# A fixed order of TensorE's instructions for the attention units of a hybrid layer

## The chip, the cores and the metric

The kernel runs on one core of a Trainium2 chip. The metric is device time in microseconds (us), the median over several runs; lower is better. One core has five engines that matter here: TensorE (PE, matmuls and transposes), VectorE (DVE), ScalarE (ACT), GpSimd (POOL) and SyncE (SP, which issues the DMAs). Each takes its instructions in the order in which the program lists them.

## The reference

One layer with four token mixers beside each other, over 640 tokens: 512 latent tokens, which see 128 cached context tokens and themselves, and 128 prompt tokens, which see only themselves. Cut to what matters:

```python
h = _rmsnorm(x, P['norm_mix_pre']) * (1 + sc1) + sh1
u = _split_cols(h @ P['w_in'])
o_a, st_a = _hgrn_mixer(u, P, lb_f, lb_b, ctx)
o_b, st_b = _swa_mixer(u, P, pos, ctx)     # windowed, 8 heads, 2 kv heads, a sink logit
o_c, st_c = _mla_mixer(u, P, pos, ctx)     # latent, 8 heads, key = 64 + 32 rotary
o_d, st_d = _gqa_mixer(u, P, pos, ctx)     # grouped, 8 heads, 2 kv heads
y = _merge((o_a, o_b, o_c, o_d), u['gates'], P)
...
# each attention: softmax(scale * q k^T) v, with the maximum taken off
# _merge: sum over branches of (o_n @ w_branch[n]) * sigmoid(gates_n), then @ w_out
```

Then the modulated MLP. Everything is float32.

## The kernel before, in words

Float32 products are made of three matmuls of a rounded high part and a rest (`wh`, `wl`, `hTh`, `hTl`), so one projection block is three lines, L365 to L367 or L381 to L383. After the start and the recurrent mixer come, in this order, windowed attention (branch 1), grouped attention (branch 3) and latent attention (branch 2), the merge, and the MLP.

Attention is done in units: two heads by 128 query rows. `unit` (L800) writes one whole unit. With 640 keys it takes each of the two heads in turn: scores into a tile `sc` of two PSUM banks (matmuls L949 and L950, in latent attention also L1182), the row maximum on VectorE (L818), the exponential with its sum on ScalarE (L819), the reciprocal on VectorE (L821) and the scaling of P on GpSimd (`weigh`, L809). With fewer keys both heads share the two banks and one reduce (L835, L840, L847). Then TensorE transposes P by pairs of key blocks (L856) into tiles `tp`, which ScalarE and VectorE copy out in turn (L858, L860) to `PT`; the products with V (L1009, in latent attention L1185) go into a tile `pv`, and `o_evac` (L504) splits it into a high part `oh` on ScalarE and a rest `ol` on VectorE. `tp` and `pv` share one pool of two PSUM banks, `pst`; the scores have `pss`, two times two banks; everything else has `psm`, two banks.

`run_gqa` (L990) does windowed and grouped attention: 20 units in two halves, with a query projection (`queries`, L906) ahead of each half; behind it `gates` (L699) makes the branch's sigmoid gates, 8 blocks of two times 24 matmuls, with a sigmoid on ScalarE after the fourth and the eighth. `merge` (L967) stands behind the gates of the branch. In `mla` (L1033) each of four head pairs has a projection of its queries, transposes of the rotary part (L1152), for every second pair the values, a projection of its keys, and then five units; after each unit three `side_steps`, pieces of the modulation (`ada`, L211) whose weights come by DMA. During latent attention `psm` is closed and its two banks hold `ada_ps` and one buffer `pj`. The unit with 128 keys is the one of the prompt.

What order the engines get is not what the code lists: outside of `in_order` (L71) a scheduler with its own timeline places each engine's instructions, so that a unit's parts stand between gates, projections and other units. Inside `in_order(PE)`, which the recurrent mixer already uses, TensorE keeps the order of the code.

## Time and profile before

| | us |
|---|---|
| median of 3 runs | 1500.1 |
| lowest, highest | 1498.42, 1501.73 |
| profiled execution, its own time | 1502.2 |
| its span | 1500.4 |
| TensorE busy | 1430.5 (95% of the span) |
| VectorE, ScalarE, GpSimd busy | 796.1, 481.4, 432.2 |
| mean granted TensorE clock | 0.991 |

TensorE's time counts matmuls and their modelled ends, so short gaps do not show as idle. A row of a timeline gives the start, the duration, the engine, line and operation, the tiles out and in, and in brackets the idle time before it with what ended it. "x4" in such a row is a run of four. A granted clock of 1.00 is 2.4 GHz, 0.50 is 1.2 GHz.

### The profile page before, as it was taken

How to read it: one execution, taken by the hardware profiler on the slowest of the kernel's cores; microseconds unless marked ns; L12 is line 12 of the kernel's file. 1: busy time of each engine (PE TensorE's matmuls, PEld its weight loads, DVE VectorE, ACT ScalarE, POOL GpSimd, SP SyncE). 2: the span in 40 equal slices, each digit the busy share in tenths (PEclk: the TensorE clock that was granted, in tenths of full speed). 3: DMA queues.
4: the chain of work that ended last, by engine and by line, in shares of the span. 5: the costliest groups of instructions: out<-in, count | busy, mean ns of one | idle time of the engine just before them, and what ended most of it. 6: DMA issues, size and time to landing. Idle time of an engine off the chain costs nothing.

```text
span 1500.4 us, 26709 instructions
## 1 busy us (share of the span) xinstructions
PE 1430.5 (95%) x10969; PEld 1302.2 (87%) x10969; DVE 796.1 (53%) x1447; ACT 481.4 (32%) x1161; POOL 432.2 (29%) x456
## 2 busy tenths in 40 slices
PE   6999999899999999999998998998999999999996
PEld 5898998899898998999996677988898998898995
DVE  4347657476643788433725566746243444444446
ACT  4334333333443235442124565225220110110112
POOL 2015325243321545222213334124111111112114
PEclk9999999999999999999999999999999999999998
DMA  9421212121112131112224601221343223222221
GB/s 328 128 85 58 70 49 64 50 68 50 45 43 59 34 84 37 33 42 74 80 68 143 224 15 43 99 85 56 112 129 101 80 71 98 71 70 71 75 66 70
DMA packets 138225, 121.17 MB, mean 81 GB/s; under 512 B 22296, under 2 KB 119412, under 8 KB 138104
## 3 DMA queue, kind: packets, MB, share of 16 engines
q1 hardware_dynamic: 138104, 119.47, 26.4%
q8 instruction: 86, 1.41, 0.4%
q14 instruction: 35, 0.29, 0.1%
HBM read 115.96 MB, written 3.49 MB: 80 GB/s over the span
## 4 chain that ended last, share of the span: by engine, by line
PE 70%; issue 13%; DVE 8%; POOL 5%; ACT 2%; DMA 1%; POOLq 0%; DVEq 0%; SPq 0%; ACTq 0%
PE mm L365 12%; PE mm L366 11%; PE mm L367 11%; PE mm L381 4%; PE mm L382 4%; PE mm L383 4%; PE tp L856 3%; POOL wh L139 3%; PE pv L1009 3%; PE sc L383 3%; PE sc L381 2%; PE sc L382 2%; PE sc L949 2%; PE sc L950 2%; DVE wl L142 1%
## 5 line engine op out<-in xcount | busy, mean ns | idle before, releaser
L139 POOL TENSOR_SCALAR wh<-wr 128x1024 fp32r<-128x1024 f32 (+3 forms) x136 | 156.7, 1154 | 536.4 <-PE mm L366 290.4
L142 DVE TENSOR_TENSOR wl<-wr,wh 128x1024 fp32r<-128x1024 f32 (+3 forms) x160 | 198.9, 1247 | 160.0 <-POOL wh L139 120.8
L365 PE MATMUL mm<-hTh,wh 128*128 128x320 f32 x704 | 220.5, 313 | 2.0 <-DVE qA L520 0.9
L367 PE MATMUL mm<-hTh,wl 128*128 128x320 f32 x704 | 219.2, 311 | 0.0
L366 PE MATMUL mm<-hTl,wh 128*128 128x320 f32 x704 | 218.2, 310 | 0.0
L366 PE MATMUL mm<-h2Tl,wh 128*128 128x320 f32 x512 | 159.4, 311 | 1.1 <-DVE h2Tl L142 1.1
L365 PE MATMUL mm<-h2Th,wh 128*128 128x320 f32 x512 | 159.5, 312 | 0.0
L367 PE MATMUL mm<-h2Th,wl 128*128 128x320 f32 x512 | 159.2, 311 | 0.0
L809 POOL TENSOR_SCALAR P<-P,rden 128x640 f32<-128x640 f32 (+3 forms) x120 | 84.5, 713 | 184.0 <-DVE rden L821 80.7
L365 PEld LDWEIGHTS mm<-hTh,wh 128*128 128x128 f32 x704 | 132.2, 188 | 3.9 <-DVE qA L520 1.0
L367 PEld LDWEIGHTS mm<-hTh,wl 128*128 128x128 f32 x704 | 132.2, 188 | 0.9 <-issue 0.7
L366 PEld LDWEIGHTS mm<-hTl,wh 128*128 128x128 f32 x704 | 132.2, 188 | 0.5 <-issue 0.3
L382 PE MATMUL mm<-wl,hidh 128*128 128x512 f32 x320 | 124.8, 390 | 0.6 <-DVE wl L142 0.6
L381 PE MATMUL mm<-wh,hidh 128*128 128x512 f32 x320 | 125.3, 392 | 0.0
L383 PE MATMUL mm<-wh,hidl 128*128 128x512 f32 x320 | 124.6, 389 | 0.0
L1292 ACT ACTIVATE relu<-mm 128x320 f32<-128x320 f32 x64 | 28.0, 438 | 281.1 <-PE mm L367 281.1
L366 PEld LDWEIGHTS mm<-h2Tl,wh 128*128 128x128 f32 x512 | 97.1, 190 | 1.7 <-DVE h2Tl L142 1.5
L365 PEld LDWEIGHTS mm<-h2Th,wh 128*128 128x128 f32 x512 | 96.9, 189 | 0.7 <-issue 0.4
L367 PEld LDWEIGHTS mm<-h2Th,wl 128*128 128x128 f32 x512 | 97.0, 189 | 0.0
L1293 DVE TENSOR_TENSOR relu<-relu 128x320 f32<-128x320 f32 x64 | 40.4, 632 | 100.8 <-ACT relu L1292 100.8
L1305 DVE TENSOR_TENSOR y<-mm,y 128x512 f32<-128x512 f32 x70 | 48.2, 689 | 81.9 <-PE mm L383 81.9
L381 PE MATMUL sc<-wh,hTh 128*128 128x256 f32 (+2 forms) x224 | 72.0, 322 | 5.5 <-DVE tx L935 2.4
(355 smaller groups left out, 3238.4 us busy)
## 6 DMA issues: line engine op xcount, KB each, us to landing
wr<-in_w_in SPq DMA_DIRECT2D x56, 512.0 KB, 3.7
wada<-in_w_ada SPq DMA_DIRECT2D x48, 512.0 KB, 4.5
wr<-in_w_mlp_in SPq DMA_DIRECT2D x32, 512.0 KB, 4.0
wr<-in_w_mlp_out SPq DMA_DIRECT2D x32, 512.0 KB, 3.6
wr<-in_w_in SPq DMA_DIRECT2D x64, 64.0 KB, 2.1
wr<-in_w_branch SPq DMA_DIRECT2D x8, 512.0 KB, 4.1
wr<-in_w_branch SPq DMA_DIRECT2D x16, 256.0 KB, 4.1
wr<-in_w_out SPq DMA_DIRECT2D x8, 512.0 KB, 3.6
```

The lines of the kernel that those rows point to most:

```text
L139: G.tensor_scalar(out=out, in0=src, scalar1=1.0, scalar2=1.0, op0=ALU.mult, op1=ALU.mult)
L142: V.tensor_tensor(out=out, in0=src, in1=f(hi), op=ALU.subtract)
L365: PE.matmul(out=ps[:, 0:tn], lhsT=wh, rhs=a, start=(k == 0), stop=False)
L366: PE.matmul(out=ps[:, 0:tn], lhsT=wh, rhs=b, start=False, stop=False)
L367: PE.matmul(out=ps[:, 0:tn], lhsT=wl, rhs=a, start=False, stop=(k == nk - 1))
L381: PE.matmul(out=ps[:, 0:n], lhsT=a, rhs=w[k][0], start=(start and k == 0), stop=False)
L382: PE.matmul(out=ps[:, 0:n], lhsT=a, rhs=w[k][1], start=False, stop=False)
L383: PE.matmul(out=ps[:, 0:n], lhsT=b, rhs=w[k][0], start=False, stop=(stop and k == nk - 1))
L809: G.tensor_scalar(out=Pt[:, i, 0:W], in0=Pt[:, i, 0:W], scalar1=rden[:, i:i + 1], scalar2=1.0, op0=ALU.mult, op1=ALU.mult)
L856: PE.transpose(out=tp[:, kk, i], in_=Pt[:, i, 128 * (kt + kk):128 * (kt + kk) + 128], identity=ident)
L1009: PE.matmul(out=out, lhsT=Vt[:, ks[kt], 64 * a:64 * a + 64], rhs=PTa, start=start, stop=stop)
L1305: V.tensor_tensor(out=ys, in0=ps, in1=ys, op=ALU.add)
```

## The change

- `unit` no longer writes its parts one after the other. It returns four functions: the first half's scores (`wide(0)`, or both halves), the second half's (`wide(1)`), the transposes in two parts (`turn`), and the products.
- `run_units` writes TensorE's order by hand, inside `in_order(PE)`. One step has the first scores of unit u, the products of unit u-2, fill, the second scores of u, transposes of u-1 (tiles 0 and 1), fill, transposes of u-1 (tile 2).
- `Fill` hands out other work by shares. In `run_gqa` the fill is the second query projection and the gates, mixed; a query transpose comes one half of a gate block after its projection. The gates are no longer behind the units.
- In `mla` all scores use one tile `scores` of three banks with one buffer: the first head of a unit in columns 0 to 639, the second in 640 to 1279. The pieces are 512+128 and 384+256 columns instead of 320+320. The projections of the next head pair are the fill beside the units of the present one, in two buffers `pj`; those of the first pair come ahead. `side_steps` are two a unit instead of three.

The core of the diff; the class `Fill`, the pools and `mla`'s inner functions, which move without change, are left out:

```diff
-        if W > 512:
-
-            for i in range(2):
-                sv = sc_tile()[:, :, 0:W // 2]
+        def wide(i):
+            if banks is None:
+
+                sv, to = sc_tile()[:, :, 0:W // 2], Pt[:, i, 0:W].rearrange("p (a n) -> p a n", a=2)
                 for a in range(2):
                     score(sv[:, a], i, a * (W // 2), W // 2)
...
+            else:
+                sv, to = banks[:, W * i:W * i + W], Pt[:, i, 0:W]
+                k0 = 0
+                while k0 < W:
+                    kn = min(W - k0, 512 - (W * i + k0) % 512)
+                    score(sv[:, k0:k0 + kn], i, k0, kn)
+                    k0 += kn
...
+        def turn(part):
+            for j, kt in list(enumerate(range(0, nk, 2)))[2 * part:2 * part + 2]:
+                kn = min(2, nk - kt)
+                tp = tp_tile().rearrange("p (k i) t -> p k i t", i=2)
+                for i in range(2):
+                    for kk in range(kn):
+                        PE.transpose(out=tp[:, kk, i], in_=Pt[:, i, 128 * (kt + kk):128 * (kt + kk) + 128], identity=ident)
+                if j % 2 == 0:
+                    S.activation(out=PT[:, kt:kt + kn], in_=tp[:, 0:kn], func=AF.Copy)
+                else:
+                    V.tensor_copy(out=PT[:, kt:kt + kn], in_=tp[:, 0:kn])
...
+        if W > 512:
+            return lambda: wide(0), lambda: wide(1), turn, products
+        return both, lambda: None, turn, products
+
+    def run_units(units, beside, after=lambda: None):
+
+
+        cur = old = None
+        units = iter(units)
+        with in_order(PE):
+            while True:
+                new = next(units, None)
+                if new is None and cur is None and old is None:
+                    break
+                if new:
+                    new[0]()
+                if old:
+                    old[3]()
+                    after()
+                beside()
+                if new:
+                    new[1]()
+                if cur:
+                    cur[2](0)
+                beside()
+                if cur:
+                    cur[2](1)
+                old, cur = cur, new
...
+        def dense():
+
+            gate = gate_steps(n, sig)
+            for i, share in enumerate(second):
+                yield share
+                if i % 2 == 0:
+                    yield next(gate)
+            yield from gate
...
+        fill = Fill(dense())
+        run_units(units(), lambda: fill.give(0.5))
+        fill.rest()
+        return sig
...
+        scores = psx.tile([128, 3, 512], F32, name="scores").rearrange("p a n -> p (a n)")
...
+        preludes = [None] + [heads(jj, got[jj], lambda: psx.tile([128, 512], F32, tag="pj", name="pj", bufs=2))
+                             for jj in range(1, 4)]
...
+        run_units(units(), lambda: fill.give(0.4), lambda: side_steps(2))
```

How this stands in the engines' orders, at three places. (`x3` is a run of three; a wait names the engine waited for; the numbers tell one buffer's use from the next.)

TensorE in grouped attention, before: the transposes of a unit. `tp_6267` is its first tile, `tp_6273` the second, `tp_6279` the third; the lines 949 and 950 are scores, 381 to 383 gates.

```order
L856 MATMUL tp_6267<-ident_82,P_6247 128x128 [waits Pool_49]
L856 MATMUL tp_6267<-ident_82,P_6247 128x128
L949 MATMUL sc_6352<-K_5397,Q_5663 128x320 [waits Activation_49]
L950 MATMUL sc_6352<-K_5397,Q_5663 128x320
...
L383 MATMUL mm_6685<-wh_6681,hTl_140 128x256
L381 MATMUL mm_6685<-wh_6681,hTh_138 128x256
L856 MATMUL tp_6273<-ident_82,P_6247 128x128 [waits Activation_49]
L856 MATMUL tp_6273<-ident_82,P_6247 128x128 x3
L856 MATMUL tp_6279<-ident_82,P_6247 128x128 [waits DVE_49]
L856 MATMUL tp_6279<-ident_82,P_6247 128x128
```

Scores of the next units and gates stand between the first tile's transposes and the second's.

TensorE in grouped attention, the change: `pv_6443` are products of unit u-2, `sc_6456` the second scores of u, `tp_6465` and `tp_6471` the first two tiles of u-1; the lines 365 to 367 are fill.

```order
L1081 MATMUL pv_6443<-PT_6198,Vt_5399 64x128 [waits Activation_49]
L1081 MATMUL pv_6443<-PT_6198,Vt_5399 64x128
L1002 MATMUL sc_6456<-K_5397,Q_5663 128x320
...
L872 MATMUL tp_6465<-ident_82,P_6345 128x128 [waits PE_49,Pool_49]
L872 MATMUL tp_6465<-ident_82,P_6345 128x128
L872 MATMUL tp_6465<-ident_82,P_6345 128x128 [waits Pool_49]
L872 MATMUL tp_6465<-ident_82,P_6345 128x128
L872 MATMUL tp_6471<-ident_82,P_6345 128x128 [waits Activation_49]
L872 MATMUL tp_6471<-ident_82,P_6345 128x128 x3
L365 MATMUL mm_6477<-hTh_137,wh_6312 128x320 [waits DVE_49]
L366 MATMUL mm_6477<-hTl_139,wh_6312 128x320
```

The second tile's transposes follow the first's at once, and wait for ScalarE.

ScalarE in grouped attention, the change, around the sigmoid of the first half of the gates (L711): `sig_6192` are the gates, L832 is the exponential, L520 is `oh`, L874 the copy of transposed tiles.

```order
L708 ACTIVATE sig_6192<-mm_7185 128x320 [waits PE_49]
L874 ACTIVATE PT_7085<-tp_7211 128x256 [waits PE_49]
L711 ACT_TABLE_LOAD
L711 ACTIVATE sig_6192<-sig_6192 128x2560 [waits Activation_49]
L832 ACT_TABLE_LOAD [waits DVE_49]
L832 ACTIVATE P_7218,den_7216<-sc_7220,negm_7215 128x640 [waits Pool_49]
L520 ACTIVATE oh_5395<-pv_7229 128x128 [waits PE_49]
L874 ACTIVATE PT_7149<-tp_7251 128x512 [waits PE_49]
L832 ACTIVATE P_7218,den_7216<-sc_7242,negm_7215 128x640 [waits DVE_49]
```

The sigmoid now stands between two table loads in the middle of the units, and behind it are the exponential of the next unit, the evacuation of products and the copy of transposed tiles.

TensorE in latent attention, the change: one step. `scores_9116` is the one tile of three banks, `pv_9269` products, L211 `ada`, `tp_9304` to `tp_9316` the three tiles of the unit before.

```order
L1002 MATMUL scores_9116<-mK_9083,mQ_9005 128x512 [waits Activation_49]
...
L1275 MATMUL scores_9116<-ckv_7858,mQ_9005 128x128
L1278 MATMUL pv_9269<-PT_9122,qv_8938 64x128 [waits DVE_49]
...
L211 MATMUL ada_ps_9117<-wada_9282,cpad_120 32x256 [waits DMAHW5_49]
L211 MATMUL ada_ps_9117<-wada_9282,cpad_120 32x256 x3
L1002 MATMUL scores_9116<-mK_9083,mQ_9005 128x384 [waits Activation_49]
...
L1275 MATMUL scores_9116<-ckv_7858,mQ_9005 128x256
L872 MATMUL tp_9304<-ident_82,P_9188 128x128 [waits PE_49,Pool_49]
...
L872 MATMUL tp_9310<-ident_82,P_9188 128x128 [waits DVE_49]
L872 MATMUL tp_9316<-ident_82,P_9188 128x128 [waits Activation_49]
L1002 MATMUL scores_9116<-mK_9083,mQ_9005 128x512 [waits Activation_49]
```

Both halves' scores are written into one tile, and each half's first matmul waits for ScalarE; products and ada steps stand between the first pair, transposes between the second.

## Rows read from the trace of the kernel before

**Rows 1.** Busy time by stage: us, PE, PEld, DVE, ACT, POOL, PEclk, DMA share, GB/s:
```profile
326.00:500.00 174.00, 168.54 (x1291) 153.95 (x1290) 97.26 (x239) 69.40 (x192) 51.67 (x71) 1.00 0.20 51
500.00:685.00 185.00, 181.35 (x1483) 172.05 (x1482) 114.00 (x250) 74.21 (x188) 67.98 (x78) 0.99 0.19 49
812.00:814.00 2.00, 2.00 (x13) 1.19 (x12) 0.96 (x2) 1.90 (x3) 0.29 (x1) 0.50 0.47 184
882.00:912.00 30.00, 24.70 (x207) 20.73 (x206) 20.76 (x47) 17.96 (x48) 14.83 (x23) 1.00 0.06 19
```

**Rows 2.** Instruction groups of PE, 326 to 500: count, busy, mean ns, idle before:
```profile
L856 PE MATMUL tp<-ident,P 128*128 128x128 f32 x120 | 20.1, 281 | 0.7 <-ACT PT L858 0.7
```

**Rows 3.** The same view, 500 to 685:
```profile
L856 PE MATMUL tp<-ident,P 128*128 128x128 f32 x168 | 25.8, 280 | 1.1 <-DVE ol L142 1.0 <-ACT PT L858 0.2
L1009 PE MATMUL pv<-PT,Vt 128*64 128x128 f32 x336 | 23.0, 279 | 1.6 <-ACT PT L858 1.6
```

**Rows 4.** Timeline of PE in windowed attention: start, duration, operation, idle before:
```profile
391.32 0.66 PE L856 MATMUL tp<-ident,P 128*128 128x128 f32 x4
392.73 0.44 PE L856 MATMUL tp<-ident,P 128*128 128x128 f32 x2 [0.75 <-ACT PT L858]
```

**Rows 5.** Timeline of PE in grouped attention:
```profile
590.99 0.66 PE L856 MATMUL tp<-ident,P 128*128 128x128 f32 x4
591.40 0.39 PE L949 MATMUL sc<-K,Q 128*128 128x320 f32 x1
...
592.40 0.66 PE L856 MATMUL tp<-ident,P 128*128 128x128 f32 x4 [0.17 <-ACT PT L858]
```

**Rows 6.** Timeline of ACT around a sigmoid:
```profile
438.80 1.28 ACT L697 ACT_TABLE_LOAD   x1
440.09 2.34 ACT L697 ACTIVATE sig<-sig 128x2560 f32<-128x2560 f32 x1
442.33 0.26 ACT L506 ACTIVATE oh<-pv 128x128 fp32r<-128x128 f32 x1
```

**Rows 7.** Timeline of PE in latent attention, products:
```profile
903.04 1.31 PE L1185 MATMUL pv<-PT,mVt 128*64 128x128 f32 x20 [0.72 <-ACT PT L858]
904.28 0.66 PE L856 MATMUL tp<-ident,P 128*128 128x128 f32 x4
...
910.25 0.88 PE L1185 MATMUL pv<-PT,mVt 128*64 128x128 f32 x12
911.05 0.44 PE L856 MATMUL tp<-ident,P 128*128 128x128 f32 x2
```

**Rows 8.** Timeline of all engines in latent attention, one half-unit:
```profile
890.52 0.79 ACT L819 ACTIVATE P<-sc,negm 128x640 f32<-128x640 f32 x1 [2.17 <-DVE negm L818]
...
891.46 0.41 PE L949 MATMUL sc<-mK,mQ 128*128 128x320 f32 x1
...
892.30 0.31 PE L1182 MATMUL sc<-ckv,mQ 128*128 128x320 f32 x1
...
892.65 0.82 DVE L818 TENSOR_REDUCE negm<-sc 128x1 f32<-128x640 f32 x1 [0.53 <-PE sc L1182]
...
893.57 0.80 ACT L819 ACTIVATE P<-sc,negm 128x640 f32<-128x640 f32 x1 [0.32 <-DVE rden L821]
```

**Rows 9.** Timeline of PE, the start of latent attention:
```profile
806.44 0.41 PE L949 MATMUL sc<-mK,mQ 128*128 128x320 f32 x1
...
810.38 0.63 PE L1182 MATMUL sc<-ckv,mQ 128*128 128x320 f32 x1 [0.58 <-POOL mQ L139]
810.82 0.47 PE L949 MATMUL sc<-mK,mQ 128*128 128x320 f32 x1
811.08 0.47 PE L950 MATMUL sc<-mK,mQ 128*128 128x320 f32 x1
```

**Rows 10.** Instruction groups of PE by form, 806 to 942, merge beside the units:
```profile
L365 PE MATMUL mm<-oh,wh 128*128 128x320 f32 x11 | 3.7, 335 | 1.4 <-DVE G L1206 1.4
```

**Rows 11.** Timeline of PE, the last products of latent attention:
```profile
941.90 0.44 PE L1185 MATMUL pv<-PT,qv 128*64 128x128 f32 x4
```

More of the change, by code (lines that the diff above doesn't have):

```diff
@@ L496, in trunk, with __init__, give, rest @@
     V.tensor_scalar(out=nsink, in0=sink_b, scalar1=-1.0, scalar2=None, op0=ALU.mult)
+    class Fill:
+        def __init__(self, steps):
+            self.steps, self.due = steps, 0.0
+        def give(self, share):
+            self.due += share
+            while self.due > 0:
+                self.due -= next(self.steps, 1e9)
+        def rest(self):
+            for _ in self.steps:
+                pass
     OT = {}
@@ L749, in trunk @@
                 for share in hgrn_out(hp, *qfk[hp], A, QP, hx):
-                    beside(share)
-            for _ in fill:
-                pass
+                    fill.give(share)
+            fill.rest()
         wtile.act = False
@@ L1140, in mla, with heads @@
         Vs += [Vs[0]]
-        for jj in range(4):
+        def heads(jj, got, bank):
             QQ = big(F32R, 4, T, name="mQ")
@@ L1160, in mla @@
                     copy_r(to[64:128], f(to[0:64]))
+                yield 0.25
             if jj % 2 == 0:
@@ new lines, in mla, with units, one, score @@
+        preludes = [None] + [heads(jj, got[jj], lambda: psx.tile([128, 512], F32, tag="pj", name="pj", bufs=2))
+                             for jj in range(1, 4)]
+        fill = Fill(iter(()))
+        def units():
+            for jj in range(4):
+                fill.rest()
+                fill.steps, fill.due = (preludes[jj + 1] if jj < 3 else iter(())), 0.0
+                for qt in range(5):
+                    yield one(jj, qt, *got[jj])
+        def one(jj, qt, Qa, QR, K):
+            ks, Vt = full_tiles(qt), Vs[jj]
+            def score(out, a, k0, kn):
+                t = slice(128 * qt, 128 * qt + 128)
+                b = slice(ks[0] * 128 + k0, ks[0] * 128 + k0 + kn)
+                qk_mm(out, Qa[a][:, t], K_part(K, b.start, kn), a, last=False)
+                PE.matmul(out=out, lhsT=QR[a][:, t], rhs=KRo[:, b], start=False, stop=True)
+            def pv_mm(out, a, kt, PTa, start, stop):
+                PE.matmul(out=out, lhsT=Vt[:, ks[kt], 64 * a:64 * a + 64], rhs=PTa, start=start, stop=stop)
+            return unit(n, jj, (0, 1), qt, len(ks), score, pv_mm, banks=scores)
```

159 lines of the change are left out of this document (75 added, 84 removed).

## The prediction

> **What bounds the kernel now.** I read the busy time by stage first [rows 1]: in windowed attention (326 to 500 us) TensorE is busy 168.5 of 174 us, in grouped attention (500 to 685) 181.4 of 185, and in a stretch of latent attention (882 to 912) 24.7 of 30. So the first two stages are bound by TensorE's own work, and only latent attention has room. Then the groups of instructions of the two full stages, to see what the rest waits for [rows 2, 3]: the transposes of the weights P wait 0.7 us in windowed attention, in grouped attention 1.1 us, and the products 1.6 us. That is all that a better order could win there from waits: 0.7 and 2.7 us. Then the timeline of single units, for what a wait costs where it does occur [rows 4, 5], and at last latent attention, its start, one half-unit and its end, in the order of its terms below.
>
> **Windowed and grouped attention: the transposes.** Before, the scheduler puts scores or gate matmuls between the first four transposes of a unit and the next ones. After, `turn(0)` issues tile 0 and tile 1 back to back, and in 10 units of each of the two stages the order shows tile 1 waiting on ScalarE: it got the PSUM buffer that ScalarE must first empty, while the other of the two holds the products just before. TensorE executes in its written order, so nothing behind can pass. The trace of before has this pattern once: four transposes start at 391.32, the next at 392.73 [rows 4]. A second place has scores between: 590.99, scores from 591.40, next transposes at 592.40 [rows 5]. Both are 1.41 us apart; four transposes alone take 0.41 (590.99 to 591.40). The wait costs 1.00 us. After has 20 of them, before one: 9 more in windowed attention, 10 in grouped. **+9.0 and +10.0 us.** The row's own idle time, 0.75 us, is the lower bound (14.3 us for the 19), since ends on TensorE are modelled.
>
> The Trainium skill has a rule against this order (Perfetto Trace Analysis, section Matmuls): independent matmul groups should rotate through different PSUM banks, so that emptying one overlaps the next. By it, with the buffers in rotation, these 19 us would be absent and the sum below would be 1499.6; with the wait as the trace shows it, it is 1518.6. The order after shows the wait, so I keep it.
>
> In 5 more units (4 in windowed, 1 in grouped attention) tile 1 waits for the products' evacuation with only tile 0 between. Bounds 0 and 1.0 us; I take 0.4, the evacuation being two short operations that start earlier: **+1.6 and +0.4.**
>
> **The sigmoid in the middle.** The gates are now fill beside the units, so the sigmoid of their first half falls between units on ScalarE, as the order shows, with the next unit's exponentials and evacuations behind it. Table load 1.28 us, sigmoid 2.34, and a table load back 1.28, taken equal to the first [rows 6]. Before had one such case too, but other matmuls ran meanwhile. In grouped attention all three and an exponential (0.8 with its accumulator read 0.2), a first evacuation (0.3) and a second (0.3) stand before the transposes' buffer is free, some 6.9 us with the transposed tile's copy, against some 2.8 us of scores, products and transposes that TensorE can still issue: **+4.1.** In windowed attention the copy stands before the second load, and the wait beyond the 1.0 already counted is about **+0.9.** Lower bound 0, where the fill covers it; upper 5 each.
>
> **What these stages gain.** Products now come in one block a unit. A block of 20 takes 1.24 us, one of 12 0.80 [rows 7], so 0.055 each and 0.14 for leaving the mode. Windowed attention goes from 35 blocks to 20: **-2.1** (at most twice that, if entering costs as much). Grouped attention goes from 21 to 20, nothing. Its present waits of 2.7 us [rows 3] go: **-2.7**; the 0.7 [rows 2] is the one that I left out of the count above. Later query transposes and `merge` written ahead of the units cost nothing: the gate matmuls hide the former, and the same matmuls only change places for the latter. Windowed +9.0+1.6+0.9-2.1 = **+9.4**; grouped +10.0+0.4+4.1-2.7 = **+11.8**.
>
> **Latent attention.** All scores lie in one tile of three banks, the second bank shared by both halves. The order shows the second half's first matmul waiting on ScalarE, and the next unit's first one as well: exponential and scores alternate. One half-unit by [rows 8]: six matmuls of 320 columns start 0.84 apart from first to last (891.46 to 892.30), the reduce starts 0.35 after the last, takes 0.82, the exponential starts 0.10 later, takes 0.79, and the next scores come 0.15 after it: 3.05 us. The new pieces (512+128, 384+256) have the same columns. A unit is 6.1 us, four of them and one of 128 keys (2 us, an estimate: shorter scores, reduce and exponentials) 26.4, four head pairs 105.6. Inside the waits lie transposes, products and two ada steps, nearly filling them. So the projections of the next pair (23 or 41 matmuls and transposes) hide only in part, and their evacuations stand in the queues of ScalarE, VectorE and GpSimd between reduce and exponential. I take 6 us for the matmuls and 7 for the queues over three pairs; bounds 0 and 25 together.
>
> The first complete score now waits for all of the first pair's projections; before, a score began at 806.44 but its third matmul came at 810.38, waiting for GpSimd [rows 9]. I take 3.9 later. The tail of the last unit, without cover, 3 us. And `merge(2)` and the gate rows (16 matmuls, and 33, of which a third is [rows 10]) no longer run beside: at 0.15 each 7.3 us. Together 3.9+105.6+6+7+3+7.3 = 132.8, against 806.44 to 941.90 [rows 9, 11], 135.5: **-2.7** (bounds -16 and +9). What was serial between head pairs before disappears, and the serialised scores take nearly all of it back.
>
> **The sum.** +9.4+11.8-2.7 = +18.5 on the profiled execution's 1502.2 us; this lies 2.1 above the median of the runs, 1500.1, so by the median **1518.6 us**.
>
> **Rivals.** *A, faster.* Latent attention reaches its floor: evacuations and projections fit inside the serial loop, -16. For the total to fall below before's, the transposes must also cost only the visible 0.75 us and the sigmoids nothing: +14.3+2.0-2.1-2.7-16 = -4.5, that is 1495.6. For it: latent attention leaves ScalarE and VectorE idle for half of its time or more. Against: three of its terms must all come out at their low ends; it decides only if latent attention wins over about 12 us. Chance 0.20.
>
> *B, no change that counts:* the transposes cost their lower bound and latent attention wins some 11 us: +14.3+2.0-2.1-2.7-11 = +0.5, 1500.6. Chance 0.08. A measurement here can tell 0.2%, 3 us, from no change.
>
> *C, slower by the clock.* TensorE's granted clock was 0.50 between 812 and 814 [rows 1], the lower of its levels of 1.2 and 2.4 GHz, after a stretch with waits for VectorE and for GpSimd; scores there start 0.26 apart (810.82 to 811.08 [rows 9]) instead of 0.17 (0.84 over five [rows 8]). If the waits of the new loop brought this down for all 16 large units, 12 scores each would cost 0.09 more: 16 x 12 x 0.09 = +17, that is 1536. Against: 882 to 912 had 18% idle and was granted 1.00 [rows 1]. Chance 0.06. The Trainium skill (TensorE: Matmul & The Clock Gate, part 1) states that the clock falls to half when the array has been idle; the row at 812 agrees, and no stretch of before is like the new loop.
>
> *D, slower by the queues:* projections' evacuations delay the loop to its upper bound, +9 instead of -2.7: 1530. For it: VectorE and ScalarE are both in the loop, and both evacuate the projections. Chance 0.11.
>
> **How the numbers follow.** The forecast case has 0.55, and its own range is 1511 to 1526: at the low end the transposes at 0.75 (-4.7) and the sigmoids at 1 each (-3.0), at the high end the sigmoids at 5 each (+5.0) and latent attention even (+2.7). With D and most of A the range is 1495 to 1531; it leaves out C and the lower part of A. Faster by over 0.2%: A, 0.20; within: B, 0.08; slower: 0.55+0.06+0.11 = 0.72.
>
> **What would show it.** In the groups of instructions after: L872 (transposes) on TensorE with some 15 us or more of idle time behind ScalarE's copies (L874), half in each stage, where before had 1.8. A gap of some 4 us on TensorE at the sigmoid in grouped attention. Large latent units about 6.1 us apart or more, with exponential, scores, reduce in turn, and no stretch without scores between head pairs. The prediction is wrong if tile 1 starts within 0.5 us of tile 0, if latent units come closer than 5.5 us, or if the stages up to 685 are not longer.

## The result, and the profile after

The change takes 1555.05 us (1549.37 to 1561.21), the kernel before 1500.65 in the same session: 1.0365 times as long, 95% interval 1.0316 to 1.0415. The forecast was 1518.6, range 1495 to 1531. The sign was right; the loss is 54 us instead of 18.5.

The profiled execution of the change took 1559.04 us. By the first instruction of each stage in its trace: the two full stages, from the first windowed score to the last of latent attention's first projections, which before all lie behind grouped attention and now partly in it, grow from 382.3 to 409.9 us (+27.6); from their end to the first latent score it is 104.7 instead of 98.1 (+6.6); latent attention, first score to last product, 156.8 instead of 135.7 (+21.1); the rest +1.4.

The windows of the change, those of [rows 1] and latent attention in pieces (columns: window and length, busy time of PE, its weight loads, DVE, ACT, POOL with counts, granted clock, DMA share, GB/s):

```profile
326.00:520.00 194.00, 176.93 (x1365) 164.04 (x1364) 102.67 (x259) 69.59 (x196) 55.00 (x77) 0.99 0.21 51
520.00:718.00 198.00, 182.42 (x1438) 171.71 (x1437) 106.86 (x230) 76.19 (x186) 62.93 (x73) 0.97 0.16 41
841.00:857.00 16.00, 11.77 (x42) 9.77 (x42) 7.78 (x16) 8.12 (x17) 5.68 (x11) 0.61 0.00 1
857.00:873.00 16.00, 14.94 (x132) 12.15 (x131) 8.47 (x18) 7.58 (x20) 6.32 (x10) 0.90 0.29 93
889.00:905.00 16.00, 15.50 (x116) 12.09 (x114) 5.64 (x12) 7.13 (x23) 3.59 (x6) 0.72 0.27 84
```

TensorE now waits in the stages that it used to fill: 17 of 194 us and 16 of 198, where [rows 1] had 5.5 and 3.6. And its clock is 0.97 in grouped attention, where [rows 1] had 0.99, and far lower in two stretches of latent attention, 0.61 and 0.72.

What it waits for, by groups of instructions on TensorE, from 326 to 520:

```profile
L872 PE MATMUL tp<-ident,P 128*128 128x128 f32 x120 | 20.7, 287 | 10.8 <-ACT PT L874 9.1 <-DVE ol L142 1.1 <-POOL P L815 0.3
```

and from 520 to 718:

```profile
L872 PE MATMUL tp<-ident,P 128*128 128x128 f32 x168 | 27.7, 281 | 12.1 <-ACT PT L874 7.7 <-DVE ol L142 4.3
...
L365 PE MATMUL mm<-oh,wh 128*128 128x320 f32 x56 | 18.9, 338 | 3.4 <-DVE sig L1033 3.4
```

The transposes wait 22.9 us where they waited 1.8 [rows 2, 3], 16.8 of them behind ScalarE's copy as the prediction said. The third row is `merge(1)`, which waited 0.6 us before. The tile named `sig` is misleading: the second sigmoid half of windowed attention was done at 491.4. Line 1033 is VectorE's product of the merge's result with the gates, which empties the merge's PSUM bank, and it stands behind the rests of two weights on VectorE:

```profile
489.03 2.34 ACT L711 ACTIVATE sig<-sig 128x2560 f32<-128x2560 f32 x1
...
534.84 2.06 DVE L142 TENSOR_TENSOR wl<-wr,wh 128x1024 fp32r<-128x1024 f32 x1
...
538.49 1.21 DVE L142 TENSOR_TENSOR wl<-wr,wh 128x1024 fp32r<-128x1024 f32 x1
539.73 0.49 DVE L1033 TENSOR_TENSOR sig<-mm,sig 128x320 f32<-128x320 f32 x1
...
540.28 0.64 PE L365 MATMUL mm<-oh,wh 128*128 128x320 f32 x1 [3.44 <-DVE sig L1033]
```

Two pairs of tile 0 and tile 1 on TensorE's timeline, and the sigmoid in grouped attention:

```profile
376.77 0.66 PE L872 MATMUL tp<-ident,P 128*128 128x128 f32 x4
378.17 0.66 PE L872 MATMUL tp<-ident,P 128*128 128x128 f32 x4 [0.75 <-ACT PT L874]
...
587.09 0.60 PE L872 MATMUL tp<-ident,P 128*128 128x128 f32 x4
588.44 0.66 PE L872 MATMUL tp<-ident,P 128*128 128x128 f32 x4 [0.75 <-ACT PT L874]
...
648.05 0.60 PE L872 MATMUL tp<-ident,P 128*128 128x128 f32 x4
652.62 1.09 PE L872 MATMUL tp<-ident,P 128*128 128x128 f32 x4 [3.96 <-DVE ol L142]
```

Tile 1 starts 1.40 and 1.35 us behind tile 0. Four transposes alone take 0.41 [rows 4, 5], so the wait costs 0.94 to 0.99: the forecast's 1.00. At the sigmoid in grouped attention it is 3.96 against a forecast of 4.1. (At the one in windowed attention, at 435.48, the row's wait is 2.51; the forecast had 1.0 and 0.9.) The bracket names VectorE, but ScalarE's timeline shows what it waited for:

```profile
645.75 0.38 ACT L874 ACTIVATE PT<-tp 128x256 f32<-128x256 f32 x1
646.15 1.28 ACT L711 ACT_TABLE_LOAD   x1
647.45 2.34 ACT L711 ACTIVATE sig<-sig 128x2560 f32<-128x2560 f32 x1
649.80 1.28 ACT L832 ACT_TABLE_LOAD   x1
651.10 0.79 ACT L832 ACTIVATE P<-sc,negm 128x640 f32<-128x640 f32 x1
651.79 0.19 ACT L832 ACTIVATION_READ_ACCUMULATOR P<-sc,negm 128x1 f32 x1
651.88 0.27 ACT L520 ACTIVATE oh<-pv 128x128 fp32r<-128x128 f32 x1
```

A split of the products (`oh`, L520) stands behind table load, sigmoid, table load and exponential, as worked out ahead; the rest `ol` and the PSUM buffer follow it.

Latent attention, a large unit of the last head pair, where no projections run beside it (all engines):

```profile
974.72 0.82 DVE L831 TENSOR_REDUCE negm<-scores 128x1 f32<-128x640 f32 x1 [1.14 <-PE scores L1275]
975.64 0.79 ACT L832 ACTIVATE P<-scores,negm 128x640 f32<-128x640 f32 x1 [1.98 <-DVE negm L831]
...
976.57 0.44 PE L1002 MATMUL scores<-mK,mQ 128*128 128x384 f32 x1 [0.65 <-ACT P L832]
...
977.76 0.82 DVE L831 TENSOR_REDUCE negm<-scores 128x1 f32<-128x640 f32 x1 [0.75 <-PE scores L1275]
...
979.68 0.50 PE L1002 MATMUL scores<-mK,mQ 128*128 128x512 f32 x1 [0.34 <-ACT P L832]
```

Scores, reduce, exponential, scores, in turn: 3.11 us from 976.57 to 979.68, against 3.05 worked out from [rows 8]. But the unit at the start of the same head pair takes 8.4 us (957.07 to 965.51), since other work stands ahead of its second reduce on VectorE:

```profile
961.98 1.23 DVE L142 TENSOR_TENSOR wl<-wr,wh 128x1024 fp32r<-128x1024 f32 x1 [0.47 <-POOL wh L139]
963.12 0.69 DVE L286 SCALAR_TENSOR_TENSOR s<-modcol,vcol 128x16 f32<-128x16 f32 x1
963.73 0.81 DVE L831 TENSOR_REDUCE negm<-scores 128x1 f32<-128x640 f32 x1
```

The half's last score matmul starts at 961.05; the reduce could start 0.35 later [rows 8], and starts at 963.73. TensorE, in its fixed order, waits 3.64 us, up to 965.51. And the step of a 128-key unit, on TensorE:

```profile
873.65 0.33 PE L1002 MATMUL scores<-Kp,mQ 128*128 128x128 f32 x1 [0.34 <-ACT P L832]
...
874.47 1.31 PE L1278 MATMUL pv<-PT,qv 128*64 128x128 f32 x20
875.71 1.07 PE L211 MATMUL ada_ps<-wada,cpad 128*32 128x256 f32 x16
876.71 1.09 PE L872 MATMUL tp<-ident,P 128*128 128x128 f32 x8
878.11 0.44 PE L872 MATMUL tp<-ident,P 128*128 128x128 f32 x2 [0.31 <-ACT PT L874]
878.31 0.48 PE L1002 MATMUL scores<-mK,mQ 128*128 128x512 f32 x1
```

Its own scores take 0.8 us, but the step also holds the products and the ten transposes of two large units and two ada steps: 4.66 us, hardly a wait in it.

### The profile page after: what moved, and what is told of

Same layout as the page of the kernel before. It is cut to its first block, busy times and chain, and to the rows that moved or that the text cites. A ratio compares the mean times of both kernels' runs of the same rounds, so it can differ in the third digit from the quotient of the medians.

```text
span 1557.2 us, 26722 instructions
## 1 busy us (share of the span) xinstructions
PE 1447.3 (93%) x10969; PEld 1319.6 (85%) x10969; DVE 793.1 (51%) x1447; ACT 480.8 (31%) x1161; POOL 431.4 (28%) x456
## 3 DMA queue, kind: packets, MB, share of 16 engines
q8 instruction: 86, 1.41, 0.4%
## 4 chain that ended last, share of the span: by engine, by line
PE 66%; issue 13%; DVE 8%; ACT 6%; POOL 5%; DMA 1%; SPq 0%; POOLq 0%; DVEq 0%; ACTq 0%
PE mm L365 11%; PE mm L366 11%; PE mm L367 11%; PE mm L381 4%; PE mm L382 4%; PE mm L383 4%; PE tp L872 3%; POOL wh L139 3%; PE sc L381 2%; PE sc L383 2%; PE sc L382 2%; PE pv L1081 2%; POOL hk L612 2%; DVE wl L142 1%; ACT P L832 1%
## 5 line engine op out<-in xcount | busy, mean ns | idle before, releaser
L872 PE MATMUL tp<-ident,P 128*128 128x128 f32 x456 | 76.2, 290 | 26.3 <-ACT PT L874 19.6
```

Of the source, the lines that this page charges most:

```text
L872: PE.transpose(out=tp[:, kk, i], in_=Pt[:, i, 128 * (kt + kk):128 * (kt + kk) + 128], identity=ident)
```

## The experiments

Times are medians of four runs (five for the last), each beside the kernel before on the same chip (1500.6 to 1502.5). A head pair is measured from its first score to its first 128-key score (four large units); in the change the four take 32.9, 35.4, 32.3 and 28.9 us, the steps between them 4.7, 6.3 and 4.8, the end 11.6.

### Which stages lose

The change for windowed and grouped attention alone, latent attention as before (the core of the edit; `whole` calls the four functions of a unit in turn, outside `in_order`):

```diff
-        run_units(units(), lambda: fill.give(0.4), lambda: side_steps(2))
...
+                whole(unit(n, jj, (0, 1), qt, len(ks), score, pv_mm))
+                side_steps(3)
```

> The fixed order in windowed and grouped attention alone; latent attention is as before. By stages the two traces differ by +11.2 us in windowed attention, +22.5 in grouped, +0.6 in the dense stretch, +21.1 in latent attention and +1.4 behind it. Theory: the stages' losses are their own, so this kernel is 34 us slower than before, about 1535, with 20 waits of 0.9 us between the first and second tile of transposes. Rival: the losses depend on each other (the latent stage is late because its inputs are, or the clock is lower after waits in the stages ahead); then it would be within 20 us of before, or above 1545.

1531.8 us, ratio 1.020 (1.0174 to 1.0226). (The expectation cuts the stages at other instructions than the section before, so its parts differ by a few us.) And latent attention's change alone:

```diff
-        run_units(units(), lambda: fill.give(0.5))
...
+                whole(unit(n, j, (j, 4 + j), qt, len(ks), score, pv_mm, sink=sink, bands=bands(qt)))
...
+    sig = gates(1)
```

> The new latent attention alone; windowed and grouped attention are in the scheduler's order. Theory: +22 us against before, about 1523. Rival, that the stages' losses depend on each other: within 10 us of before.

1525.4 us, ratio 1.0165 (1.0147 to 1.0183). +30.8 and +24.4 make 55, the whole loss. By stages, too, the parts hardly touch each other: latent attention takes 134.6 us in the first run (135.7 before), the two full stages 383.9 in the second (382.3 before). Latent attention, forecast at -2.7, loses nearly as much as the other two.

### Windowed and grouped attention

All of the fill between tile 0 and tile 1 of the transposes, so that no tile stands directly behind the one whose copy it waits for:

```diff
-            for j, kt in list(enumerate(range(0, nk, 2)))[2 * part:2 * part + 2]:
+            first = 1 if banks is None else 2
+            for j, kt in list(enumerate(range(0, nk, 2)))[first * part:[first, None][part]]:
...
-        run_units(units(), lambda: fill.give(0.5))
+        run_units(units(), lambda: fill.give(1.0), early=lambda: None)
```

> The change with one edit in windowed and grouped attention: all fill of a step goes between the first tile of transposes and the second. Theory: the 20 waits of 0.9 us are paid only because nothing stands between; they go, and the time falls by 18 us against the change, to about 1537. Rival: the wait moves to the next instruction that needs one of the two buffers (the second tile against the third, or the products); then less than 6 us is gained, 1549 or more.

1541.0 us (1538.6 to 1542.9), 14 below the change. From 520 to 722 of its trace:

```profile
L873 PE MATMUL tp<-ident,P 128*128 128x128 f32 x168 | 25.1, 276 | 0.6 <-POOL P L815 0.4 <-ACT PT L875 0.2
...
L1082 PE MATMUL pv<-PT,Vt 128*64 128x128 f32 x336 | 23.3, 279 | 2.3 <-ACT PT L875 2.1
L365 PE MATMUL mm<-oh,wh 128*128 128x320 f32 x56 | 18.5, 331 | 3.7 <-DVE sig L1034 3.7
```

In grouped attention the transposes' wait of 12.1 us is gone; the sigmoid's stall is now at the products (2.1), and `merge(1)` waits as before. In windowed attention the wait behind ScalarE's copies goes too (9.1 to 0.5), but another takes most of its place, for GpSimd's scaling of P. From 328 to 520:

```profile
L873 PE MATMUL tp<-ident,P 128*128 128x128 f32 x120 | 21.9, 287 | 8.0 <-POOL P L815 7.2 <-ACT PT L875 0.5
```

Both stages together take 397.8 us, 12 less; the time, 14 less, lies between the 18 of the theory and the 6 of the rival. The mechanism of the transposes is shown in both stages; what it costs is regained in grouped attention, and in windowed attention mostly not, by this edit.

The sigmoids. The first attempt listed both behind the units:

```diff
-            if kk % 4 == 3:
+            if kk % 4 == 3 and n in (0, 2):
                 S.activation(out=g, in_=g, func=AF.Sigmoid)
...
         fill.rest()
+        for g in sig:
+            S.activation(out=g, in_=g, func=AF.Sigmoid)
         return sig
```

> The changed kernel with one edit: both sigmoids of a branch's gates stand behind all of its units. Theory (the stalls at the sigmoid in the middle, 2.7 and 4.1 us, are its table loads and its length): these go, and since merge(1) in any case waits for the second half, its wait of 3.6 us becomes up to 6: 3 to 5 us below the change, 1550 to 1552. Rival (the stalls only move: the two sigmoids in a row hold the copies and evacuations of the last units and merge by as much): within 2 us of the change.

1555.0 us (1549.6 to 1563.2). ScalarE's order is not fixed, and the scheduler put both sigmoids back to where they were: it is the change a second time and says nothing on the sigmoids. It served for the clock, below. With a dependency that holds them behind the last evacuation:

```diff
+        traced = nc.cur_bb.bb.instructions
+        last = next(i for i in reversed(traced) if i.engine == S.engine)
         for g in sig:
             S.activation(out=g, in_=g, func=AF.Sigmoid)
+            new = next(i for i in reversed(traced) if i.engine == S.engine)
+            tc.add_manual_dep(new, last.name, ...)
+            last = new
```

> As the run before meant it: both sigmoids of a branch now stand behind the last unit's evacuation on ScalarE, held there by a dependency, in windowed and grouped attention. Theory (the stalls at the middle sigmoid, 2.7 and 4.1 us, are the table loads and the sigmoid on ScalarE): from the first windowed score to the last of the latent projections ahead (409.6 us in the change) 5 to 6 us less, because merge(1) waits no longer than now for its sigmoids. Rival (the wait only moves to merge(1), which then waits for both sigmoids): less than 3 us less there.

1552.4 us. From the first windowed score to the last of the projections 405.7 us, 4.2 less: between the two expectations. From 515 to 735:

```profile
L872 PE MATMUL tp<-ident,P 128*128 128x128 f32 x168 | 27.2, 278 | 8.9 <-ACT PT L874 8.4 <-DVE ol L142 0.3
L365 PE MATMUL mm<-oh,wh 128*128 128x320 f32 x70 | 22.1, 316 | 2.3 <-DVE sig L1033 2.3
```

In grouped attention the 4 us behind `ol` went; in windowed attention the stall moved, since grouped attention's first evacuations now stand behind two sigmoids (TensorE waits 6.3 us up to 499, where it waits 2.0 in the change). That `merge(1)` waits for its sigmoids, as both expectations have it, is not so (see the profile after); its wait is VectorE's, 2.3 us here.

The fixed order itself: `run_units` lists the same parts, and the scheduler orders TensorE again, in all three stages.

```diff
-        with in_order(PE):
+        if True:
             while True:
                 new = next(units, None)
```

> The changed kernel without the fixed order: run_units lists the same parts, but the scheduler places TensorE's instructions again, in all three stages; pools, three banks, fill and pieces stay. Theory 1 (the fixed order is what costs windowed and grouped attention their 31 us): latent attention's first transposes come near 685 again (719 in the change), and since all latent scores still share one tile that must be emptied half by half, latent attention keeps some 15 of its 21 us: 1515 to 1520. Rival (the parts themselves cost it, late products, late query transposes, gates beside the units): both stages stay 20 us or more longer, 1540 or more.

1540.2 us (1539.8 to 1544.0), 15 below the change: the rival's time, but not its stages. The two full stages take 395.8 us, 14 less than the change and 13.5 more than before. Of the transposes' waits behind ScalarE's copies one is left, 2.7 us in windowed attention; besides it there are a clock of 0.97 over both stages, `merge(1)`'s wait of 3.4 us, and the end of grouped attention. From 679 to 692:

```profile
L1081 PE MATMUL pv<-PT,Vt 128*64 128x128 f32 x40 | 3.7, 341 | 3.2 <-ACT PT L874 2.6 <-DVE PT L876 0.6
L1002 PE MATMUL sc<-K,Q 128*128 128x320 f32 x4 | 2.0, 509 | 1.2 <-ACT P L832 1.2
```

The last gate matmul starts at 678, and the last two units have no cover; the scores' mean goes to 509 ns, the lower clock. In the kernel before, gate matmuls last to 685, the end of the stage.

### Latent attention

Without fill: the next pair's projections between the pairs, in the fixed order.

```diff
-        run_units(units(), lambda: fill.give(0.4), lambda: side_steps(2))
+        run_units(units(), lambda: None, lambda: side_steps(2))
```

> The change with the projections of head pairs 1 to 3 written between the pairs instead of beside the units. In the change the head pairs take 37.6, 41.7, 37.0 us with projections beside and 28.9 without, so the projections cost 29.6 us there. Theory 1: put into the serial loop they delay reduce and exponential and are hidden hardly at all; written in a row between the pairs they cost about 11 us each, as before, so the time changes by less than 6 us (1549 to 1561). Theory 2: most of their matmuls are hidden beside the units and the 29.6 us are the clock: then taking them out adds some 20 us, about 1575.

1590.2 us (1585.7 to 1593.2), beyond both. The four head pairs take 30.5, 29.3, 27.6 and 28.4 us, but the steps between them 16.7, 20.6 and 20.3: the projections wait one by one for their own evacuations there. So beside the units they cost the change 32.9-30.5, 35.4-29.3, 32.3-27.6 and 28.9-28.4, 13.7 us together (the last pair has none in either run). And four large units cost 29 us without any projections, not 24.4.

More work for TensorE beside the units, to raise its clock:

```diff
+        def warm():
+            fill.give(0.4)
+            pad = psx.tile([128, 512], F32, tag="pj", name="pad", bufs=2)
+            for _ in range(5):
+                PE.matmul(out=pad[:, 0:256], lhsT=KRo[:, 0:128], rhs=KRo[:, 0:256], start=True, stop=True)
-        run_units(units(), lambda: fill.give(0.4), lambda: side_steps(2))
+        run_units(units(), warm, lambda: side_steps(2))
```

> The change with five matmuls of 256 columns more at each of the two places for fill in a unit of latent attention; they compute nothing that is used and only keep TensorE busy, 0.6 us a place. Theory: the granted clock of 0.61 to 0.9 in the first units of a head pair costs more than these matmuls; then the clock of the stage rises to 0.95 or more and the time falls by 5 us or more against the change. Rival: the stage waits for the chain of reduce and exponential, and the clock costs little; then the time is equal or up to 15 us longer.

1581.1 us, 26 above the change, beyond both. Latent attention's window in this run:

```profile
845.20:1010.90 165.70, 141.68 (x1220) 119.92 (x1221) 73.07 (x161) 70.85 (x193) 50.58 (x76) 0.93 0.27 90
```

in the change:

```profile
840.70:997.50 156.80, 132.30 (x1046) 104.54 (x1048) 76.96 (x167) 71.87 (x194) 51.23 (x76) 0.87 0.28 95
```

and in the change's second run, above:

```profile
839.40:988.40 149.00, 123.53 (x1046) 97.61 (x1048) 77.02 (x167) 71.49 (x194) 51.92 (x76) 0.94 0.30 100
```

The last two rows are one order of instructions: 7.8 us more at a granted clock of 0.87 than at 0.94. The first row is 16.7 us longer than the third at a like clock, and it no longer holds the 37 gate-row and merge matmuls that stood before the last products. From the first latent score to the end of the kernel, where all work is in, it is 25.0 us more (733.5 to 708.5) for 220 added matmuls, 0.114 each where the expectation had 0.12: they are paid nearly in full. They fill the waits for exponentials, but they write into the projections' buffers and wait for these to be emptied, 15.6 us. In the same window:

```profile
L1284 PE MATMUL pad<-ckv 128*128 128x256 f32 x210 | 36.9, 308 | 15.6 <-DVE mQ L1226 8.7 <-DVE mQ L784 4.2 <-DVE mK L142 1.8
```

So the run does not tell what the clock alone would be worth.

A smaller share of the projections, spread over all units of a pair:

```diff
+                share[0] = 0.31 if jj == 1 else 0.16
...
-        run_units(units(), lambda: fill.give(0.4), lambda: side_steps(2))
+        run_units(units(), lambda: fill.give(share[0]), lambda: side_steps(2))
```

> The change with the projections spread evenly over the ten places of a head pair (shares 0.16 and 0.31 instead of 0.4). Theory: they cost so much because two or more pieces stand in the first half-unit and their evacuations in front of the reduce and the exponential; spread, 8 to 15 us are gained, 1540 to 1547. Rival: every piece delays the chain by its own evacuation wherever it stands; then the time is within 5 us of the change.

1553.2 us (1552.5 to 1555.4): no gain. Then the shared bank: the halves in two tiles of two banks, as before the change, for which one of the two projection buffers had to go.

```diff
-        scores = psx.tile([128, 3, 512], F32, name="scores").rearrange("p a n -> p (a n)")
+        scores = [psx.tile([128, 2, 512], F32, name="scores%d" % i) for i in range(2)]
...
-    psx.tile([128, 512], F32, tag="pj", name="pj", bufs=2)
+    psx.tile([128, 512], F32, tag="pj", name="pj", bufs=1)
```

> The change with the two score halves of latent attention in two tiles of two banks each (320+320 columns again), and one projection buffer instead of two. Theory 1: the shared bank serialises scores and exponentials, which makes a large unit 6.3 us where nothing else is beside; with own banks such a unit needs about 5.0 us and the latent stage, 157 us, falls by 16 x 1.3, about 20 us, total about 1535. Theory 2: the projections' evacuations in the queues and the lower clock make the latent stage long; then a unit without projections still gains, but in all less than 8 us, 1547 or more.

1558.7 us (1557.0 to 1561.4): nothing gained, which the first theory did not allow. But a large unit in the last pair:

```profile
975.24 0.39 PE L999 MATMUL scores<-mK,mQ 128*128 128x320 f32 x1
...
977.54 0.41 PE L999 MATMUL scores<-mK,mQ 128*128 128x320 f32 x1
...
980.00 0.39 PE L999 MATMUL scores<-mK,mQ 128*128 128x320 f32 x1
```

4.76 us instead of 6.2, and that pair takes 19.9 us instead of 28.9. The pairs with projections beside take 33.1, 42.2 and 34.4, up to 7 more than in the change. Was it the one buffer? The change with one buffer and its three banks kept:

```diff
-    psx.tile([128, 512], F32, tag="pj", name="pj", bufs=2)
+    psx.tile([128, 512], F32, tag="pj", name="pj", bufs=1)
```

> The change with one buffer for the projections in latent attention instead of two; the scores' three banks and everything else stay. It splits the run with own banks for the halves, which came out at the change's time. Theory (own banks do help in the fixed order, but the single projection buffer took it back): latent attention 8 to 20 us longer than the change's 149 to 157, 1563 to 1575 in all. Rival (the single buffer costs little, and own banks gain nothing in the fixed order): within 4 us of the change.

1573.9 us (1571.7 to 1578.2), as the theory said: by the medians the buffer is worth 19 us in the fixed order, and own banks give 15 of them back (1573.9 to 1558.7). Some 4 of the 19 lie ahead of latent attention, where nothing was edited. In latent attention the matmuls into `pj` wait 22.9 us, in the change 1.9. Own banks without fill, two of the edits above together:

```diff
+        scores = [psx.tile([128, 2, 512], F32, name="scores%d" % i) for i in range(2)]
...
+        run_units(units(), lambda: None, lambda: side_steps(2))
```

> Own banks for the two score halves, as in the run before, and no projections beside the units. There the last head pair, without projections, took 20 us instead of 28.9, and those with projections 38 to 47. Theory: the shared bank costs 8 to 9 us a head pair, and what hid that in the run with own banks is the single projection buffer, on which TensorE waits in its fixed order; without projections beside, four pairs gain 8 us each, about 1523. Rival: the gain of the last pair was its high clock and the missing ada steps; then less than 12 us is gained, 1543 or more.

1581.8 us, 8.5 below the run without fill alone and far above the first figure: the pairs fall to 21.3, 25.3, 25.0 and 21.4 us, but the steps between them grow to 21.4, 31.5 and 23.1 with one buffer. And own banks with the scheduler's order, in all stages:

```diff
+        scores = [psx.tile([128, 2, 512], F32, name="scores%d" % i) for i in range(2)]
...
-        with in_order(PE):
+        if True:
```

> The same without the fixed order, and the latent scores' halves in two tiles of two banks each (one buffer for the projections instead of two). Theory 1 (the loss is the fixed order plus the shared banks): everything is back at the kernel before or below it, 1493 to 1503, because the projections beside the units can now fill the waits. Rival (the single projection buffer and its evacuations hold latent attention, whoever sets the order): 1512 or more.

1518.3 us (1516.4 to 1520.3), ratio 1.0102 (1.0087 to 1.0117), the rival's time, yet latent attention is not held by its one buffer here. Its window in the run of free order with shared banks (columns as in the first windows):

```profile
828.70:977.40 148.70, 127.65 (x1032) 90.92 (x1033) 74.67 (x166) 72.11 (x193) 49.14 (x74) 0.98 0.30 100
```

and with own banks:

```profile
827.70:958.00 130.30, 119.36 (x1043) 91.23 (x1042) 75.16 (x167) 71.66 (x194) 48.70 (x74) 0.98 0.35 114
```

With the clock the same, 0.98, the shared bank costs 18.4 us, although the run with own banks has one projection buffer less. Own banks in a free order need 5.4 less than before's 135.7. (The rest of the 1518.3 is the two full stages, 14 us longer, and the first score, 7 later.)

| latent scores, projection buffers | fixed order | free order |
|---|---|---|
| three shared banks, two | 1555.05 | 1540.2 |
| three shared banks, one | 1573.9 | not run |
| own banks, one | 1558.7 | 1518.3 |

Latent attention alone in the traces of these runs, with its granted clock (the change has two traces):

| latent scores, projection buffers | fixed order | free order |
|---|---|---|
| three shared banks, two | 156.8 (0.87), 149.0 (0.94) | 148.7 (0.98) |
| three shared banks, one | 172.7 (0.84) | not run |
| own banks, one | 155.1 (0.88) | 130.3 (0.98) |

So the 15 us that the free order gives with shared banks are nearly all in the two full stages (14). In latent attention it gives next to nothing against the change's second trace; only together with own banks does it bring latent attention below before's 135.7, and the last run, below, did not repeat that.

The last run put together what these point to: the two full stages as before, latent attention with own banks in a free order, and the first pair's values behind its queries and keys.

```diff
-        for _ in heads(0, got[0], lambda: banks.reverse() or banks[0]()):
-            pass
...
+        for _ in range(6):
+            next(first)
...
+        for _ in first:
+            pass
```

(The first six steps are queries, rotary part and keys; the rest are the values, in the buffer of the other pairs.)

> What the runs point to: windowed and grouped attention as before, latent attention with the scores' halves in two tiles of two banks, without the fixed order, the next pair's projections beside the units; and the first pair's values behind the first pair's queries and keys, so that its scores need not wait for them. Theory (both the fixed order and the shared banks cost latent attention its time, and the stages do not touch each other): first score at about 810, latent attention 128 to 131 us where before had 136, the rest as before: 1497 to 1503. Rival (the free order won in the run before only because TensorE came late to this stage, with weights and evacuations long ready): latent attention 136 or more, 1506 to 1512.

1514.4 us (1513.7 to 1516.7), ratio 1.0077 (1.0063 to 1.0091): the time is beyond both ranges. The first score comes at 810, as expected, but latent attention takes 142.7 us, the rival's 136 or more, at a clock of 0.92. From 808 to 953, the ada steps' group:

```profile
L211 PE MATMUL ada_ps<-wada,cpad 128*32 128x256 f32 x192 | 19.4, 456 | 4.1 <-DMA wada<-in_w_ada 3.9
```

and the window from 840 to 856:

```profile
840.00:856.00 16.00, 12.08 (x104) 5.74 (x103) 4.97 (x12) 4.69 (x12) 4.47 (x8) 0.78 0.83 289
```

From 842 to 858 no score is issued; ada steps and the next pair's projections stand there, and the DMA engines are 83% busy. But the ada steps' wait is only 1 us more than in the run with own banks and free order throughout (4.1 to 3.0). Of the 12.4 us more in latent attention (142.7 to 130.3), TensorE's idle time makes 2.8 and its busy time 9.6 (129.0 to 119.4), at a clock of 0.92 instead of 0.98 and with 21 more matmuls on record. So the weights that come late are at most a small part by their waits; whether they brought the clock down is not shown, and another place for them was not tried. No version run here beats the kernel before; a second projection buffer beside own banks has no bank left, and was not tried either.

## Why the prediction was wrong

**Windowed and grouped attention: +27.6 instead of +21.2, by the mechanism named.** The transposes' wait, forecast at 1.00, is 0.94 to 0.99, and 12 us went when fill stood between the tiles, mostly in grouped attention. The row's idle time of 0.75, taken as the lower bound, did fall short. The Trainium skill (Perfetto Trace Analysis, section Matmuls) says that groups should rotate through PSUM banks; the trace agrees, at about 1 us for each that does not. The sigmoid in grouped attention was right (4.1 to 3.96), the one in windowed attention low (0.9 beyond the 1.0; the row has 2.51). The `ol` waits were forecast at 2.0; the rows leave at most 1.4 beside the sigmoid. Missing were 2.8 us more of `merge(1)`'s wait for VectorE (0.6 to 3.4), because I checked where `merge` stands on TensorE and not what stands ahead of its product on VectorE, and the clock: TensorE is busy 4 us more over both stages (377.25 to 373.19) for the same matmuls, at 0.98 instead of 1.00, though the fewer product blocks should have taken 2.1 off.

**Latent attention: the failing step is "A unit is 6.1 us, four of them and one of 128 keys (2 us, an estimate ...) 26.4, four head pairs 105.6", and "the tail of the last unit, without cover, 3 us".** The loop was right: exponential and scores alternate, 3.11 us a half where nothing disturbs it. But I multiplied one clean half-unit by 32. The four pairs of the run without fill average 29.0 us, 7.2 a large unit, 18 us more over 16 of them. Two things in it are shown: the clock (7.8 us over the stage between two traces of one order) and VectorE's queue, where weights of the next stage delay a reduce by 2.3 us and TensorE cannot pass. How the 18 divide between them is not settled. The 128-key step was priced by its scores; it also carries the products, transposes and ada steps of the units before, TensorE's own time: 4.7, 6.3 and 4.8 us. With the end at 11.6 these make 27.4 us where the sum had 11 (four times 2, and 3). The large units, with their projections, come to 129.5 where it had 110.6.

**Right, or nearly, in latent attention:** the projections beside the units, forecast at 13, cost 13.7. "Nearly filling them" held, too: in the clean unit above TensorE waits only 0.65 and 0.34 us before its two halves. The first score was forecast 3.9 later and came 6.6 later. `merge(2)` and the gate rows, forecast at 7.3, cost 1.4 at most behind the last product: 16 gate-row and 21 merge matmuls still stand ahead of it, within the 11.6 of the end, so that part of what the end has too much is theirs. So 18.9 (large units) + 16.4 (128-key steps and end) + 2.7 (first score) - 5.9 = 32.1 too little, which takes -2.7 to +29.4; by the stages it is +29.1.

**The rivals.** *A* and *B* needed latent attention to win 11 to 16 us; it lost. *C* was the nearest: the half clock came, in part of the units, and with it time. It was priced at 17 for all large units and given 0.06, because 882 to 912 of the kernel before was granted 1.00 with 18% idle; the new loop's stretch at 841, with 26% idle, was granted 0.61. How far the clock falls is not settled by the order, though: in the change's second trace the same stretch, 839.7 to 855.7, has 31% idle and was granted 0.89. The Trainium skill (TensorE: Matmul & The Clock Gate, part 1) says the clock halves when the array has idled. The trace agrees in that both low stretches begin behind waits (3.21 us at 840.73; 0.42 and 1.41 before 887.64). *D*, evacuations in the queues, did not reach its bound: the projections cost 13.7 of at most 25, and spreading them changed nothing, though a single buffer for them costs 16 to 24 us in latent attention. The range's high end, 1531, had D alone (C, 1536, was left out of it), and not the two full stages and latent attention off together.

**Deeper than the sum:** in the two full stages the bound that I did not price is that TensorE, once its order is fixed, passes on the delays of ScalarE and VectorE; the same parts in a free order take 14 us less there (409.9 to 395.8). In latent attention the fixed order alone is not the cause. The shared bank holds it in either order (148.7 us free; 149.0 and 156.8 fixed; 135.7 before), and the single projection buffer that own banks need holds it in the fixed order (155.1). With own banks and a free order it is 130.3 in one run and 142.7 in another, which reaches the stage earlier. I had priced the shared bank by one clean turn of its loop.

## What to carry to other kernels

Before fixing an engine's order by hand, follow each instruction to what it needs from engines whose order stays free: a sigmoid, a weight's rest or a late reduce that a scheduler would have stepped around becomes idle time. A loop is priced by its mean under the whole stage's queues and clock, not by its cleanest turn, and a short unit in a pipeline costs what the long units before it leave to it. Halves that alternate between two engines want PSUM banks of their own, and the projections beside them a second buffer; a change that bought one with the other gained nothing here in a fixed order (1558.7 to 1555.05). An edit with two parts is tried one by one and together: here neither own banks nor a free order alone brought latent attention below 148, and the two together did.

## What was not expected of the hardware

One order of instructions, run eight times (the change and its second run), took 1549.4 to 1563.2 us, and its mean granted clock goes with it: 0.985 at 1549.4, 1549.6 and 1549.7, 0.983 at 1551.1, 0.976 and 0.975 at 1559.0 to 1561.2, 0.973 at 1563.2. The kernel before, which fills TensorE, stays within about 6 us in each session. A stage with waits can pay for them a second time, by the clock of the matmuls that follow: in the stretch at 841 twelve projection matmuls start 0.27 us apart, at 889 to 905 TensorE is busy 97% of the time and still at 0.72, behind waits of 0.42 and 1.41 us. What makes one execution lower than the other is not shown. It also reaches stages that an edit leaves alone: in the run with one projection buffer the two full stages take 413.0 us instead of 409.9 with the same waits (32.6 us in both traces, TensorE busy 380.3 instead of 377.3), so single runs that differ by 3 to 4 us in all say little here.
